# Weight splitting spread over an attention layer's ticks, low parts one block behind, and a differential layer with its memory units first

## The chip, the cores and the metric

The kernel runs on one core of a Trainium2 chip. The metric is the device time of one execution in microseconds. Before the change the median of three runs is 2098.37 us (2098.26 to 2100.83).

## The reference

A transformer of two blocks runs in fp32 on one sequence of 256 rows, width 1024. Cut to what matters here:

```python
def first_block(x, mem, ...):
    mem_n = rmsnorm(mem, mem_norm_g)
    for i in range(2):
        kv = mem_n @ mem_w_kv[i]                                # memory keys and values
        x = x + 0.5 * swiglu(rmsnorm(x, ...), ffn_w_up[i, 0], ffn_w_down[i, 0])
        h = rmsnorm(x, norm_g[i, 1])
        mix = pool_layer(h, ...) if i == 0 else diff_layer(h, ...)
        x = x + mix
        x = x + 0.5 * swiglu(rmsnorm(x, ...), ffn_w_up[i, 1], ffn_w_down[i, 1])
    return rmsnorm(x, final_norm_g)

def diff_layer(h, w_in, lam_p, norm_g, w_out, mem_k, mem_v, slopes, layer_idx):
    proj = h @ w_in                                             # q, k, v, xq
    o = diff_attention(q, k, v, lam, slopes)                    # softmax(c=0) - lam * softmax(c=1), times v
    o = rmsnorm(o, norm_g, eps=SUBLN_EPS) * (1.0 - lam_init)
    xo = memory_attention(xq, mem_k, mem_v)
    return jnp.concatenate([o, xo], axis=-1) @ w_out
...
```

A second block follows: attention with block-sparse heads and heads that keep the top 64 keys by an index score, with a modulation of its norms that comes out of a matrix `w_ada`, and then a layer of product-key experts (the query phase finds the top 16 keys of each half, the expert phase runs over all experts' matrices u and v).

## The kernel before, in words

The program is one straight list of instructions; `manual_schedule` (line 63) keeps the order in which the code emits them on each engine. Nothing is moved by a scheduler, so where a line stands in a generator decides what it waits behind.

**Weights.** Every matrix is stored in blocks of 512 KB (128 x 1024 fp32). `load_to` (L120) issues their loads on SP's queue, five blocks ahead. fp32 products are made of three fp32r matmuls (`mm3`, L184 to L186: high by high, high by low, low by high), so each block is split: `split_one` (L131) lets ACT copy the high part (`whi`, L144) and DVE subtract it from the raw block for the low part (`wlo`, L145). `nextw` (L150) hands out one block and before that splits up to four blocks ahead; `fetch(4)` hands out four, a group's worth, so the four blocks of the next group are split in one burst.

**Order around the change.** In the feed-forward layers a group is `proj_cols` over four blocks: 96 matmuls, with an evacuation by DVE in the middle (`silu`, L520 to L522) and one at the end (`gate`, L532); the next group's `fetch(4)` comes behind that. In the first three feed-forward layers, pieces of `w_ada` stand between the weight blocks in the list `items`; when their turn comes to be split, `ada_piece` (L454) runs two DVE operations instead (`acc`, L463 and L465).

In the pool layer, the differential layer and the second block's attention, `pipeline(units, order)` walks over units (an attention head pair of one row tile each, or a memory head pair) in ticks; a unit is a list of steps s0, s1, ... (scores, softmax, transposes, products), and each tick runs one step of several units in the order given by the second argument. Between ticks a table `counts` says how many yields of the chain `fill` (projections, then the output rows `out_proj_k`) to run. The differential layer fills k0 and q0 first, runs the differential units over k1, q1, v and xq, and ends with the memory units (`mem_units`, L548).

**Names in the rows.** mm and sm are PSUM tiles of matmuls, tr of transposes; hT is the layer's transposed input; mT the transposed memory; cat the concatenated outputs before the output matrix; e a softmax tile; score and m belong to the top-k rounds; sc, v and i to the top-16 jobs of the query phase.

```python
def mm3(out, a, b, start, stop):
    PE.matmul(out, a[0], b[0], start=start, stop=False)
    PE.matmul(out, a[0], b[1], start=False, stop=False)
    PE.matmul(out, a[1], b[0], start=False, stop=stop)
...
drain(qk(k[0]), qk(q[0]))
units = [make(t, h) for g in range(2) for t in range(NT) for h in (4 * g, 4 * g + 2)]
units += mem_units(sp, qx, n4.rstd, KT[1], VV[1], ..., ("k0", "q0", "k1", "q1"))
```

Of the kernel before, what the change touches and what calls it, by code (L numbers as in the profile page):

```python
# [60 lines left out]
def kernel(ctx: ExitStack, tc: tile.TileContext, A, LAY, stop=None):  # L61
# [38 lines left out]


    items = []
    st = {"load": 0, "split": 0, "use": 0, "nsplit": 0, "raw": {}, "s": {}}
    deferred = []
    cfg = {"raw": 5, "ahead": 4}
    CH = 1024
    wpool = ctx.enter_context(pool("wp", side="right"))
    wstack = ctx.enter_context(ExitStack())
# [11 lines left out]
    def load_to(n):  # L120
        while st["load"] < min(n, len(items)):
# [6 lines left out]
            st["raw"][st["load"]] = r  # L128
            st["load"] += 1

    def split_one():  # L131
        j = st["split"]
        load_to(j + cfg["raw"])
        _, nk, w, call = items[j][:4]
        n = nk * w
        r = st["raw"].pop(j)
        if call is not None:
            call(r[:, :n].rearrange("p (k w) -> p k w", w=w))
        else:
            p_ = wpool2 if j < dense and st["nsplit"] % 2 else wpool  # L140
            st["nsplit"] += 1
            hi = p_.tile([P, CH], F32R, name="whi", tag="whi", bufs=4)
            lo = p_.tile([P, CH], F32R, name="wlo", tag="wlo", bufs=4)
            ACT.activation(hi[:, :n], r[:, :n], AF.Copy)  # L144
            V.tensor_tensor(lo[:, :n], r[:, :n], hi[:, :n].bitcast(F32), op=OP.subtract)  # L145
            st["s"][j] = Split(hi[:, :n].rearrange("p (k w) -> p k w", w=w), lo[:, :n].rearrange("p (k w) -> p k w", w=w))
        st["split"] += 1
        load_to(j + 1 + cfg["raw"])

    def nextw():  # L150
        while items[st["use"]][3] is not None:
            st["use"] += 1
        j = st["use"]
        ahead, k = 0, j + 1
        while k < len(items) and ahead < cfg["ahead"]:
            ahead += items[k][3] is None
            k += 1
        while st["split"] < k:
            split_one()
        st["use"] += 1  # L160
        return st["s"].pop(j), items[j][1], items[j][2]

    def split_more(n):
        for _ in range(n):
# [59 lines left out]
    def proj_cols(act, n, n_ct, evac):  # L224
        got = fetch(n)
        for c0 in range(0, n_ct, 2):
            p = pmm()
            m = min(2, n_ct - c0)
            for j in range(m):
                if j:  # L230
                    yield
                proj_col(act, got, c0 + j, p[:, j * S:(j + 1) * S])
            evac(c0, m, p[:, :m * S].rearrange("p (j t) -> p j t", t=S))
            yield
        run_deferred()

# [157 lines left out]
    def out_proj_k(segs, update, nxt, tail=2, ahead=None):  # L394


        p = [[pmm() for _ in range(2)] for _ in range(NT)]
        n = len(segs)

        def mm(t, h, gis, gots):  # L400
            for gi in gis:
                act, k0 = segs[gi]
                for c, k, _ in gots[gi][h]:
                    mm3(p[t][h], act[:, k0 + k, t * P:(t + 1) * P], c[:, k, :], gi == 0 and k == 0, gi == n - 1 and k == 1)

        gots = {}
        for gi in range(n - tail):
            gots[gi] = [fetch(1), fetch(1)]
            for t in range(NT):
                for h in range(2):  # L410
                    mm(t, h, [gi], gots)
                if t:
                    run_deferred()
                yield
        was = dict(cfg)
        cfg.update(ahead=8 - 2 * tail)
        for gi in range(n - tail, n):
            gots[gi] = [fetch(1), fetch(1)]
        cfg.update(was)
        for t in range(NT):  # L420
            for h in range(2):
                cut = n - 1 if nxt.deep and t and h else n
                mm(t, h, range(n - tail, cut), gots)
                if cut < n:
                    was = dict(cfg)
                    cfg.update(ahead=0)
                    ahead.append(fetch(4))
                    nxt.realT(0)
                    mm(t, h, range(cut, n), gots)
                    if tail > 2:  # L430
                        split_more(1)
                update(t, h, p[t][h])
                nxt.pre(t, h)
                if not nxt.deep and (t or h):
                    nxt.T(*((0, 0), (0, 1), (1, 0))[2 * t + h - 1])
                if h:
                    nxt.stats(t)
                if cut < n:
                    ahead.append(fetch(4))
                    cfg.update(was)  # L440
                yield
        if not nxt.deep:
            nxt.late = [lambda: nxt.T(1, 1)]
# [101 lines left out]

    XS = 128 ** -0.5

    def mem_units(sp, qT, rstd, kT, v, dst, tags):  # L548

        turn = itertools.cycle(tags)  # L550

        def make(hp, t):
            e = {}

            def s0():
# [6 lines left out]
                mx, nb, sm, rc = (small([P, 2], x, bufs=6) for x in ("mx", "nb", "sum", "rc"))  # L562
                V.tensor_reduce(mx, pv, axis=AX.X, op=OP.max)
                V.tensor_scalar(nb, mx, rs, -1.0, op0=OP.mult, op1=OP.mult)
                ee = sp.tile([P, 2, S], F32, name="e", tag=next(turn), bufs=1)
                for j in range(2):
                    ACT.activation(ee[:, j], pv[:, j], AF.Exp, bias=nb[:, j:j + 1], scale=rs, accum_out=sm[:, j:j + 1])
                e["e"], e["s"], e["r"] = ee, sm, rc
# [181 lines left out]
        return dump(xt)  # L750

    n2 = Norm(A["norm_g"][0, 2])
    with pool("pl") as sp:
        cat = Split(sp.tile([P, 12, S], F32R, name="cat_hi"), sp.tile([P, 12, S], F32R, name="cat_lo"))
        pb = sp.tile([P, 4, 384], F32, name="poolB")
# [6 lines left out]
        def u_part(h):  # L762
            got = fetch(4)
            for t in range(NT):
                n1.before(t)
                p = pmm()
                rows_mm(p, hT, got[:4], t, 0, 512, 8)
                yield
                rows_mm(p, hT, got[4:], t, 0, 512, 8)
                ACT.activation(u[t][:, h * 512:(h + 1) * 512], p, AF.Copy, scale=n1.rstd[:, t:t + 1])  # L770
                if t:
                    run_deferred()
                yield

        def pooled(c0):
# [8 lines left out]
        def mixed():  # L784
# [4 lines left out]
            for ct in range(8):  # L789
                g, db = ct // 2, ct % 2  # L790
                p = psm()[:, :S]
                for cb in range(2):
                    col = cb * S + db * P
                    mm3(p, wg[g][0][:, g % 2, col:col + P], hT[:, 2 * g + cb, :], cb == 0, cb == 1)
                split_evac(cat[:, ct, :], p, psc[:, ct:ct + 1])
                if ct % 2:
                    yield

        drain(u_part(0), proj_cols(hT, 4, 4, lambda c0, m, p: ACT.activation(qT[:, c0:c0 + m, :], p, AF.Copy)))
# [3 lines left out]
        for n, _ in zip(counts, pipeline(units, [(1, 2), (3, 3), (None, 0), (0, 0), (2, 2)])):  # L803
            for _ in range(n):
                step(fill)
        drain(fill)
    kv0.close()
    if stop == "pool":
        return dump(xt)
# [9 lines left out]


    n5 = Norm(A["norm_g"][1, 2])
    with pool("df") as sp:
        cat = Split(sp.tile([P, 12, S], F32R, name="cat_hi"), sp.tile([P, 12, S], F32R, name="cat_lo"))
        nd = sp.tile([P, S], F32, name="nd")
# [97 lines left out]
        def v_part(h):  # L922

            got = fetch(4)
            for t in range(NT):
                n4.before(t)
                p = pmm()
                rows_mm(p, hT, got[:4], t, 0, 512, 8)
                yield
                rows_mm(p, hT, got[4:], t, 0, 512, 8)  # L930
                ACT.activation(v[:, t, h * 512:(h + 1) * 512], p, AF.Copy, scale=n4.rstd[:, t:t + 1])
                if t:
                    run_deferred()
                yield

        drain(v_part(0))
# [2 lines left out]
        def qk(dst):  # L939
            return proj_cols(hT, 4, 4, lambda c0, m, p: V.tensor_tensor(dst[:, c0:c0 + m, :], p, rbb, op=OP.mult))  # L940

        drain(qk(k[0]), qk(q[0]))
        units = [make(t, h) for g in range(2) for t in range(NT) for h in (4 * g, 4 * g + 2)]
        units += mem_units(sp, qx, n4.rstd, KT[1], VV[1], Split(cat.hi[:, 8:, :], cat.lo[:, 8:, :]), ("k0", "q0", "k1", "q1"))
        o = out_proj_k([(cat, i) for i in range(0, 12, 2)], plain_add, n5)
        fill = itertools.chain(qk(k[1]), qk(q[1]), v_part(1),
                               proj_cols(hT, 4, 4, lambda c0, m, p: ACT.activation(qx[:, c0:c0 + m, :], p, AF.Copy)), o)
        counts = [1] * 9 + [2, 0, 1, 0, 0, 2, 1, 1, 1, 0, 0] + [1, 0] * 2 + [1, 1, 0, 1, 0, 2]
        for i, _ in enumerate(pipeline(units, [(5, 6), (1, 2), (4, 4), (None, 0), (6, 6), (0, 0), (3, 3), (2, 2)])):
            for _ in range(counts[i] if i < len(counts) else 1):  # L950
                step(fill)
        drain(o)
    kv1.close()
    if stop == "diff":
        return dump(xt)
# [45 lines left out]
        return dump(xt)  # L1001


    gotv, got = m1.got
    mvp = [pmm() for _ in range(NT)]
    iqp, ixp = pmm(), psm()
# [93 lines left out]
    def v_part():  # L1100
        got = fetch(4)
        for t in range(NT):
            p = pmm()
            rows_mm(p, hT, got[:4], t, 0, 512, 8)
            yield
            rows_mm(p, hT, got[4:], t, 0, 512, 8)
            ACT.activation(av[:, t, 512:], p, AF.Copy)
            if t:
                run_deferred()
            yield  # L1110

    def make(t, g):
# [88 lines left out]
        return dump(xt)  # L1201


    got = m2.got
    def q_rows(b, t):
        p = pmm()
# [87 lines left out]
    for f in late_scores:  # L1294
        f()
    q1st.close()
    wstack.close()
    pq2 = pqst.enter_context(pool("pq2"))

# [252 lines left out]
def _np_layout(inputs):  # L1552
# [36 lines left out]
    lay["pool_w_group"] = [(0, 2, 512), (P * 1024, 2, 512)]  # L1589
    pack("pool_w_out", g["pool_w_out"][0], None, order=range(6))  # L1590
    w = g["diff_w_in"][0]
    pack("diff_w_in", np.concatenate([w[:, 2048:2560], w[:, 1024:1536], w[:, :512], w[:, 1536:2048], w[:, 512:1024], w[:, 2560:]], 1),
         [512] * 7)
    pack("diff_w_out", g["diff_w_out"][0], None, order=range(6))
    pack("w_ada", g["w_ada_2"][0], [512] * 12)
    w = g["w_in_2"][0]
    w = np.concatenate([w[:, 1024:1536], w[:, 3072:], w[:, :1024], w[:, 1536:3072]], 1)
# [37 lines left out]
```

## Time and profile before

| | us |
|---|---|
| median of three runs | 2098.37 |
| the profiled execution | 2098.71 |
| its span | 2096.9 |
| PE busy | 2033.5 |
| DVE busy | 1458.4 |
| ACT busy | 985.5 |

The span runs from the first to the last instruction; the execution's time is 1.8 us longer. The stages in the trace, by their start: memory keys and values 0, first feed-forward layer 48, pool layer 279, two feed-forward layers 375, differential layer 780, fourth feed-forward layer 875, the second block's norm 1088 and attention 1122, query phase 1260, expert phase 1318. To read such a profile, look first at how busy TensorE is in each stage, then at what it waits for where it isn't, and then, on the engine that releases it, at what stood ahead of the late instruction. The mean granted TensorE clock of the execution is 0.987.

### The profile page before, as it was taken

What the parts mean: (1) busy time and instruction counts of PE and PEld (TensorE: products, weight loads), DVE (VectorE), ACT (ScalarE), POOL (GpSimd) and SP (SyncE); (2) the same over time, 40 slices, a digit from 0 to 9 for tenths busy, and PEclk for the clock granted to TensorE, in tenths of its full rate; (3) what the DMA queues carried; (4) which work ended last, traced back from release to release, by engine and by line L of the source; (5) the groups of instructions that cost most, each with busy time, mean ns of one, the idle gap of its engine ahead of it and who ended that gap; (6) DMA issues with size and microseconds to landing.
All of it is one profiled execution on the core that took longest, in us unless ns stands there. A gap on an engine that the chain in (4) does not pass through costs nothing. (4 is left out here: it accounts for less than half of the span.)

```text
span 2096.9 us, 34488 instructions
## 1 busy us (share of the span) xinstructions
PE 2033.5 (97%) x13678; PEld 1832.0 (87%) x13678; DVE 1458.4 (70%) x2330; ACT 985.5 (47%) x1508; POOL 39.0 (2%) x74
## 2 busy tenths in 40 slices
PE   8999999999999998899989899999999999999998
PEld 7999888998999797799878779999998888888886
DVE  6677566776677568756658688889976666666666
ACT  6444454444444445354444344455554444444444
POOL 2000000000000000000000000000000000000000
PEclk9999999999999999999999899999999999999999
DMA  7667535676576552355545333556676776777764
GB/s 274 217 236 266 188 134 205 227 250 233 185 248 244 187 195 101 120 191 198 206 124 180 104 98 134 175 178 213 245 252 209 226 231 207 225 243 225 225 211 140
DMA packets 142379, 416.93 MB, mean 199 GB/s; under 512 B 12469, under 2 KB 47429, under 8 KB 140041
## 3 DMA queue, kind: packets, MB, share of 16 engines
q1 hardware_dynamic: 102672, 372.04, 52.4%
q10 hardware_dynamic: 37976, 36.91, 5.5%
q0 software_dynamic: 1568, 5.77, 0.9%
q8 instruction: 107, 1.75, 0.3%
q14 instruction: 56, 0.45, 0.1%
HBM read 396.82 MB, written 17.86 MB: 198 GB/s over the span
## 5 line engine op out<-in xcount | busy, mean ns | idle before, releaser
L145 DVE TENSOR_TENSOR wlo<-raw,whi 128x1024 fp32r<-128x1024 f32 (+1 forms) x654 | 780.6, 1222 | 329.8 <-ACT whi L144 329.5
L144 ACT ACTIVATE whi<-raw 128x1024 fp32r<-128x1024 f32 (+1 forms) x654 | 663.0, 1048 | 147.6 <-PE mm L186 85.4
L184 PE MATMUL mm<-hT_hi,whi 128*128 128x256 f32 x1680 | 479.9, 286 | 0.0
L185 PE MATMUL mm<-hT_lo,whi 128*128 128x256 f32 x1680 | 473.1, 282 | 0.0
L186 PE MATMUL mm<-hT_hi,wlo 128*128 128x256 f32 x1680 | 472.9, 281 | 0.0
L184 PEld LDWEIGHTS mm<-hT_hi,whi 128*128 128x128 f32 x1680 | 319.0, 190 | 6.5 <-issue 6.1
L185 PEld LDWEIGHTS mm<-hT_lo,whi 128*128 128x128 f32 x1680 | 318.9, 190 | 2.0 <-issue 1.9
L186 PEld LDWEIGHTS mm<-hT_hi,wlo 128*128 128x128 f32 x1680 | 318.7, 190 | 0.0
L184 PE MATMUL sm<-hT_hi,whi 128*128 128x256 f32 (+1 forms) x1048 | 299.5, 286 | 5.4 <-DVE hT_hi L192 2.2
L186 PE MATMUL sm<-hT_hi,wlo 128*128 128x256 f32 (+1 forms) x1048 | 296.5, 283 | 4.4 <-DVE wlo L145 4.4
L185 PE MATMUL sm<-hT_lo,whi 128*128 128x256 f32 (+1 forms) x1048 | 296.1, 283 | 0.4 <-DVE hT_lo L195 0.4
L184 PEld LDWEIGHTS sm<-hT_hi,whi 128*128 128x128 f32 (+1 forms) x1048 | 199.2, 190 | 8.7 <-DVE hT_hi L192 2.6
L184 PE MATMUL mm<-whi,wh 128*128 128x512 f32 x512 | 204.1, 399 | 2.1 <-ACT wh L194 2.1
L186 PEld LDWEIGHTS sm<-hT_hi,wlo 128*128 128x128 f32 (+1 forms) x1048 | 199.2, 190 | 4.8 <-DVE wlo L145 4.8
L186 PE MATMUL mm<-whi,wl 128*128 128x512 f32 x512 | 202.2, 395 | 0.0
L185 PEld LDWEIGHTS sm<-hT_lo,whi 128*128 128x128 f32 (+1 forms) x1048 | 199.3, 190 | 2.8 <-DVE hT_lo L195 0.6
L185 PE MATMUL mm<-wlo,wh 128*128 128x512 f32 x512 | 201.5, 394 | 0.0
L194 ACT ACTIVATE wh<-wf 128x256 fp32r<-128x256 f32 x128 | 53.5, 418 | 215.6 <-DVE wf L1484 215.6
L184 PE MATMUL mm<-whi,gT_hi 128*128 128x512 f32 x352 | 140.0, 398 | 0.0
L186 PE MATMUL mm<-whi,gT_lo 128*128 128x512 f32 x352 | 139.5, 396 | 0.0
L185 PE MATMUL mm<-wlo,gT_hi 128*128 128x512 f32 x352 | 138.6, 394 | 0.0
L1316 ACT ACTIVATE act<-sm 128x256 f32<-128x256 f32 x128 | 49.1, 384 | 166.3 <-PE sm L186 166.3
(308 smaller groups left out, 2615.9 us busy)
## 6 DMA issues: line engine op xcount, KB each, us to landing
raw<-in_ffn_up_dram SPq DMA_DIRECT2D x176, 512.0 KB, 5.2
raw<-in_peer_u_dram SPq DMA_DIRECT2D x128, 512.0 KB, 3.7
raw<-in_peer_v_dram SPq DMA_DIRECT2D x128, 512.0 KB, 3.8
raw<-in_ffn_dn_dram SPq DMA_DIRECT2D x88, 512.0 KB, 5.2
raw<-in_w_ada_dram SPq DMA_DIRECT2D x48, 512.0 KB, 5.0
gall<-stage ACTq DMA_DIRECT2D x16, 1024.0 KB, 4.6
G<-gall ACTq DMA_DIRECT2D x16, 1024.0 KB, 7.2
raw<-in_diff_w_in_dram SPq DMA_DIRECT2D x28, 512.0 KB, 5.5
```

What stands on the lines that cost most here:

```text
L144: ACT.activation(hi[:, :n], r[:, :n], AF.Copy)
L145: V.tensor_tensor(lo[:, :n], r[:, :n], hi[:, :n].bitcast(F32), op=OP.subtract)
L184: PE.matmul(out, a[0], b[0], start=start, stop=False)
L185: PE.matmul(out, a[0], b[1], start=False, stop=False)
L186: PE.matmul(out, a[1], b[0], start=False, stop=stop)
L194: ACT.activation(hi, src, AF.Copy)
L1316: ACT.activation(act[n], p, AF.Gelu)
```

## The change

Three edits.

1. Everywhere, `split_one` emits only the high part and notes the block in `st["low"]`; the low part of a block is emitted one block later (`low_one`), or at once when the item split is a piece of `w_ada`, or when `nextw` hands out the block. The prefetch runs as many blocks shorter as there are low parts open.
2. In the pool layer, the differential layer and the second block's attention `cfg["spread"]` is set: `nextw` splits nothing ahead, and `ahead_one()` at each yield of the projections and output rows splits one block, at most four ahead.
3. In the differential layer the xq projection and the memory units come first, the differential units after; the columns of `diff_w_in` and rows of `diff_w_out` are packed in the new order, and `counts` is new.

```diff
+    def low_one():
+        j, r, p_ = st["low"].pop(0)
+        c = st["s"][j]
+        nk, w = items[j][1:3]
+        lo = p_.tile([P, CH], F32R, name="wlo", tag="wlo", bufs=4)
+        V.tensor_tensor(lo[:, :nk * w], r[:, :nk * w], c.hi.rearrange("p k w -> p (k w)").bitcast(F32), op=OP.subtract)
+        c.lo = lo[:, :nk * w].rearrange("p (k w) -> p k w", w=w)
...
     def split_one():
         j = st["split"]
-        load_to(j + cfg["raw"])
+        load_to(j + cfg["raw"] - len(st["low"]))
...
             hi = p_.tile([P, CH], F32R, name="whi", tag="whi", bufs=4)
-            lo = p_.tile([P, CH], F32R, name="wlo", tag="wlo", bufs=4)
             ACT.activation(hi[:, :n], r[:, :n], AF.Copy)
-            V.tensor_tensor(lo[:, :n], r[:, :n], hi[:, :n].bitcast(F32), op=OP.subtract)
-            st["s"][j] = Split(hi[:, :n].rearrange("p (k w) -> p k w", w=w), lo[:, :n].rearrange("p (k w) -> p k w", w=w))
+            st["s"][j] = Split(hi[:, :n].rearrange("p (k w) -> p k w", w=w), None)
+            st["low"].append((j, r, p_))
         st["split"] += 1
-        load_to(j + 1 + cfg["raw"])
+        while len(st["low"]) > 1 or st["low"] and call is not None:
+            low_one()
+        load_to(j + 1 + cfg["raw"] - len(st["low"]))
...
-        while k < len(items) and ahead < cfg["ahead"]:
+        while k < len(items) and ahead < cfg["ahead"] and not cfg["spread"]:
...
         while st["split"] < k:
             split_one()
+        while st["s"][j].lo is None:
+            low_one()
...
+    def ahead_one():
+        if cfg["spread"] and st["split"] < min(st["use"] + 4, len(items)):
+            split_one()
...
                 if j:
+                    ahead_one()
                     yield
...
-        drain(qk(k[0]), qk(q[0]))
-        units = [make(t, h) for g in range(2) for t in range(NT) for h in (4 * g, 4 * g + 2)]
-        units += mem_units(sp, qx, n4.rstd, KT[1], VV[1], Split(cat.hi[:, 8:, :], cat.lo[:, 8:, :]), ("k0", "q0", "k1", "q1"))
-        o = out_proj_k([(cat, i) for i in range(0, 12, 2)], plain_add, n5)
-        fill = itertools.chain(qk(k[1]), qk(q[1]), v_part(1),
-                               proj_cols(hT, 4, 4, lambda c0, m, p: ACT.activation(qx[:, c0:c0 + m, :], p, AF.Copy)), o)
-        counts = [1] * 9 + [2, 0, 1, 0, 0, 2, 1, 1, 1, 0, 0] + [1, 0] * 2 + [1, 1, 0, 1, 0, 2]
+        drain(proj_cols(hT, 4, 4, lambda c0, m, p: ACT.activation(qx[:, c0:c0 + m, :], p, AF.Copy)))
+        units = mem_units(sp, qx, n4.rstd, KT[1], VV[1], Split(cat.hi[:, 8:, :], cat.lo[:, 8:, :]), ("e",), 6)
+        units += [make(t, h) for g in range(2) for t in range(NT) for h in (4 * g, 4 * g + 2)]
+        o = out_proj_k([(cat, i) for i in (8, 10, 0, 2, 4, 6)], plain_add, n5)
+        fill = itertools.chain(qk(k[0]), qk(q[0]), qk(k[1]), qk(q[1]), v_part(1), o)
+        counts = [1] * 16 + [1, 1, 1, 0, 1, 1, 1, 1, 0, 1, 1, 0, 1, 1, 0, 1] + [1, 0, 1, 1]
...
+    while st["low"]:
+        low_one()
     wstack.close()
```

The order that comes of it, at three places (the changed kernel's lines are shifted: L145 is now L137, L465 is L488, L532 is L555, L680 and L683 are L703 and L706, L1090 and L1091 are L1122 and L1123).

DVE at the start, while the first memory group waits for its weights; before:

```order
4 L680 TENSOR_TENSOR xg<-tr,cols 128x512 x2
5 L145 TENSOR_TENSOR wlo<-raw,whi 128x1024
6 L683 TENSOR_TENSOR mT_lo<-xg,mT_hi 128x4x128
7 L680 TENSOR_TENSOR xg<-tr,cols 128x512
8 L683 TENSOR_TENSOR mT_lo<-xg,mT_hi 128x4x128
9 L680 TENSOR_TENSOR xg<-tr,cols 128x512
10 L683 TENSOR_TENSOR mT_lo<-xg,mT_hi 128x4x128 x2
11 L145 TENSOR_TENSOR wlo<-raw,whi 128x1024 x3
```

and now:

```order
4 L703 TENSOR_TENSOR xg<-tr,cols 128x512 x2
5 L706 TENSOR_TENSOR mT_lo<-xg,mT_hi 128x4x128
6 L703 TENSOR_TENSOR xg<-tr,cols 128x512
7 L706 TENSOR_TENSOR mT_lo<-xg,mT_hi 128x4x128
8 L703 TENSOR_TENSOR xg<-tr,cols 128x512
9 L706 TENSOR_TENSOR mT_lo<-xg,mT_hi 128x4x128 x2
10 L137 TENSOR_TENSOR wlo<-raw,whi 128x1024 x4
```

The first low part has moved from ahead of the four mT_lo to behind them.

DVE at a group's end in the first feed-forward layer, where a piece of `w_ada` is next; before:

```order
L507 TENSOR_TENSOR gT_lo_698<-gate_921,gT_hi_697 128x512
L532 TENSOR_TENSOR gate_1056<-mm_1007,silu_924 128x512
L465 SCALAR_TENSOR_TENSOR acc_797<-raw_929,cols_79,acc_797 128x512 x2
L145 TENSOR_TENSOR wlo_1065<-raw_933,whi_1064 128x1024
L145 TENSOR_TENSOR wlo_1071<-raw_939,whi_1070 128x1024
L145 TENSOR_TENSOR wlo_1077<-raw_945,whi_1076 128x1024
```

and now:

```order
L530 TENSOR_TENSOR gT_lo_694<-gate_917,gT_hi_693 128x512
L555 TENSOR_TENSOR gate_1052<-mm_1003,silu_920 128x512
L488 SCALAR_TENSOR_TENSOR acc_793<-raw_931,cols_79,acc_793 128x512 x2
L137 TENSOR_TENSOR wlo_1058<-raw_925,whi_943 128x1024
L137 TENSOR_TENSOR wlo_1068<-raw_933,whi_1064 128x1024
L137 TENSOR_TENSOR wlo_1074<-raw_941,whi_1066 128x1024
```

Behind the piece now stands the low part of a block whose high part (`whi_943`) was made in the burst before. PE takes that block as the last of the four of the group it has just begun:

```order
564 L203 MATMUL mm_1088<-hT_lo_68,whi_937 128x256
565 L204 MATMUL mm_1088<-hT_hi_67,wlo_945 128x256
566 L202 MATMUL mm_1088<-hT_hi_67,whi_943 128x256 [waits Activation_49]
567 L203 MATMUL mm_1088<-hT_lo_68,whi_943 128x256
568 L204 MATMUL mm_1088<-hT_hi_67,wlo_1058 128x256 [waits DVE_49]
569 L202 MATMUL mm_1088<-hT_hi_67,whi_943 128x256
```

DVE in the second block's attention, between the top-k rounds (four MAX and four MATCH_REPLACE each) that follow the index score; before, the second round and what follows it:

```order
690 L1090 MAX m_11303<-score 128x8
691 L1091 MATCH_REPLACE score<-m_11303,score 128x128
692 L1090 MAX m_11306<-score 128x8
693 L1091 MATCH_REPLACE score<-m_11306,score 128x128
694 L1090 MAX m_11309<-score 128x8
695 L1091 MATCH_REPLACE score<-m_11309,score 128x256
696 L1090 MAX m_11312<-score 128x8
697 L1091 MATCH_REPLACE score<-m_11312,score 128x256
698 L145 TENSOR_TENSOR wlo<-raw,whi 128x1024 x4
```

and now:

```order
704 L1118 TENSOR_TENSOR score<-score,fut 128x256
705 L137 TENSOR_TENSOR wlo<-raw,whi 128x1024
706 L1122 MAX m_11256<-score 128x8
707 L1123 MATCH_REPLACE score<-m_11256,score 128x128
708 L1122 MAX m_11259<-score 128x8
709 L1123 MATCH_REPLACE score<-m_11259,score 128x128
710 L1122 MAX m_11262<-score 128x8
711 L1123 MATCH_REPLACE score<-m_11262,score 128x256
712 L1122 MAX m_11265<-score 128x8
713 L1123 MATCH_REPLACE score<-m_11265,score 128x256
714 L137 TENSOR_TENSOR wlo<-raw,whi 128x1024
```

Four low parts in a row have become one between each two rounds.

## Rows read from the trace of the kernel before

**Rows 1.** The page, part 1: busy us (share of the span) of each engine, instructions.
```profile
PE 2033.5 (97%) x13678; PEld 1832.0 (87%) x13678; DVE 1458.4 (70%) x2330; ACT 985.5 (47%) x1508; POOL 39.0 (2%) x74
```

**Rows 2.** Windows: stretch and its length, busy us (instructions) by engine, PEclk, DMA share, GB/s.
```profile
50.00:279.00 229.00, 229.00 (x1578) 211.63 (x1577) 152.02 (x182) 101.58 (x125) 2.17 (x4) 1.00 0.64 222
...
279.00:375.00 96.00, 93.62 (x548) 81.33 (x548) 65.20 (x100) 49.46 (x77) 2.65 (x3) 1.00 0.47 161
...
780.00:875.00 95.00, 81.04 (x502) 69.98 (x501) 73.53 (x179) 45.96 (x128) 4.07 (x4) 0.95 0.29 100
...
1122.00:1260.00 138.00, 125.25 (x784) 104.84 (x782) 109.90 (x255) 60.14 (x131) 2.60 (x3) 0.93 0.37 122
...
1260.00:1318.00 58.00, 52.85 (x390) 50.25 (x391) 50.61 (x252) 24.66 (x34) 0.43 (x1) 0.97 0.36 126
```

**Rows 3.** Waits of PE, whole span: engine line waited for, total us, times, longest.
```profile
PE tr L243 <- DVE cat_lo L201: 5.1, 2, 4.3
...
PE sm L186 <- DVE wlo L145: 4.4, 2, 3.9
...
PE tr L243 <- DVE e L1152: 3.8, 1, 3.8
...
PE tr L243 <- DVE qr L1256: 1.5, 1, 1.5
```

**Rows 4.** Windows again: two stretches right behind long waits.
```profile
1173.90:1180.70 6.80, 6.80 (x28) 5.96 (x29) 5.16 (x15) 2.08 (x8) 0.00 (x0) 0.50 0.41 145
...
1314.00:1317.30 3.30, 3.09 (x14) 3.09 (x15) 3.30 (x9) 0.00 (x0) 0.00 (x0) 0.50 0.68 191
```

**Rows 5.** Timeline of DVE at the start: start us, us, operation, count, [idle <-releaser].
```profile
8.88 1.23 DVE L145 TENSOR_TENSOR wlo<-raw,whi 128x1024 fp32r<-128x1024 f32 x1 [1.64 <-ACT whi L144]
...
12.42 1.47 DVE L683 TENSOR_TENSOR mT_lo<-xg,mT_hi 128x512 fp32r<-128x512 f32 x2
```

**Rows 6.** Timeline of PE at the start.
```profile
11.53 0.63 PE L185 MATMUL mm<-wlo,mT_hi 128*128 128x512 f32 x1
```

**Rows 7.** Timeline of PE: matmul 21 of the first kT group.
```profile
26.25 0.28 PE L186 MATMUL mm<-mT_hi,wlo 128*128 128x256 f32 x1
```

**Rows 8.** Timeline of DVE around the same group.
```profile
27.96 0.15 DVE L249 TENSOR_SCALAR ms<-ss 128x1 f32<-128x1 f32 x1
```

**Rows 9.** Timeline of DVE at a group end in the first feed-forward layer.
```profile
95.14 0.68 DVE L532 TENSOR_TENSOR gate<-mm,silu 128x512 f32<-128x512 f32 x1
...
95.74 1.53 DVE L465 SCALAR_TENSOR_TENSOR acc<-raw,cols,acc 128x512 f32<-128x512 f32 x2
```

**Rows 10.** Timeline of PE there: first matmul of the next group, and its matmul 21.
```profile
94.96 0.28 PE L184 MATMUL mm<-hT_hi,whi 128*128 128x256 f32 x1
...
97.31 0.28 PE L186 MATMUL mm<-hT_hi,wlo 128*128 128x256 f32 x1
```

**Rows 11.** The page, part 5 (mean ns of one) and part 6 (us to landing).
```profile
L145 DVE TENSOR_TENSOR wlo<-raw,whi 128x1024 fp32r<-128x1024 f32 (+1 forms) x654 | 780.6, 1222 | 329.8 <-ACT whi L144 329.5
...
raw<-in_ffn_up_dram SPq DMA_DIRECT2D x176, 512.0 KB, 5.2
```

**Rows 12.** Timeline of DVE in the differential layer.
```profile
816.47 4.63 DVE L145 TENSOR_TENSOR wlo<-raw,whi 128x1024 fp32r<-128x1024 f32 x4 [0.78 <-ACT whi L144]
```

**Rows 13.** Timeline of PE right behind it.
```profile
822.69 0.66 PE L243 MATMUL tr<-ident,e 128*128 128x128 f32 x2 [4.26 <-DVE cat_lo L201]
```

**Rows 14.** Timeline of DVE in the second block's attention: two successive top-k rounds.
```profile
1130.23 0.29 DVE L1090 MAX8 m<-score 128x8 f32<-128x128 f32 x1
...
1133.38 0.28 DVE L1090 MAX8 m<-score 128x8 f32<-128x128 f32 x1
```

**Rows 15.** Timeline of PE in the same microseconds.
```profile
1134.90 0.28 PE L186 MATMUL mm<-hT_hi,wlo 128*128 128x256 f32 x1
```

**Rows 16.** Timeline of DVE in the query phase: first index searches of two successive jobs.
```profile
1283.46 0.29 DVE L1230 FIND_INDEX8 i<-v,sc 128x8 uint32<-128x128 f32 x1
...
1288.13 0.29 DVE L1230 FIND_INDEX8 i<-v,sc 128x8 uint32<-128x128 f32 x1
```

More of the change, by code (lines that the diff above doesn't have):

```diff
@@ L102 @@
     items = []
-    st = {"load": 0, "split": 0, "use": 0, "nsplit": 0, "raw": {}, "s": {}}
+    st = {"load": 0, "split": 0, "use": 0, "nsplit": 0, "raw": {}, "s": {}, "low": []}
     deferred = []
-    cfg = {"raw": 5, "ahead": 4}
+    cfg = {"raw": 5, "ahead": 4, "spread": False}
     CH = 1024
@@ L233, in proj_cols @@
             evac(c0, m, p[:, :m * S].rearrange("p (j t) -> p j t", t=S))
+            ahead_one()
             yield
@@ L413, in out_proj_k @@
                     run_deferred()
+                ahead_one()
                 yield
@@ L440, in out_proj_k @@
                     cfg.update(was)
+                if not nxt.deep:
+                    ahead_one()
                 yield
@@ L546, with mem_units @@
     XS = 128 ** -0.5
-    def mem_units(sp, qT, rstd, kT, v, dst, tags):
+    def mem_units(sp, qT, rstd, kT, v, dst, tags, bufs=1):
         turn = itertools.cycle(tags)
@@ L564, in s0 @@
                 V.tensor_scalar(nb, mx, rs, -1.0, op0=OP.mult, op1=OP.mult)
-                ee = sp.tile([P, 2, S], F32, name="e", tag=next(turn), bufs=1)
+                ee = sp.tile([P, 2, S], F32, name="e", tag=next(turn), bufs=bufs)
                 for j in range(2):
@@ L752 @@
     n2 = Norm(A["norm_g"][0, 2])
+    cfg["spread"] = True
     with pool("pl") as sp:
@@ L767, in u_part @@
                 rows_mm(p, hT, got[:4], t, 0, 512, 8)
+                ahead_one()
                 yield
@@ L772, in u_part @@
                     run_deferred()
+                ahead_one()
                 yield
@@ L796, in mixed @@
                 if ct % 2:
+                    ahead_one()
                     yield
@@ L806 @@
         drain(fill)
+    cfg["spread"] = False
     kv0.close()
@@ L821 @@
     n5 = Norm(A["norm_g"][1, 2])
+    cfg["spread"] = True
     with pool("df") as sp:
@@ L928, in v_part @@
                 rows_mm(p, hT, got[:4], t, 0, 512, 8)
+                ahead_one()
                 yield
@@ L933, in v_part @@
                     run_deferred()
+                ahead_one()
                 yield
@@ L952 @@
         drain(o)
+    cfg["spread"] = False
     kv1.close()
@@ L1001 @@
         return dump(xt)
+    cfg["spread"] = True
     gotv, got = m1.got
@@ L1104, in v_part @@
             rows_mm(p, hT, got[:4], t, 0, 512, 8)
+            ahead_one()
             yield
@@ L1109, in v_part @@
                 run_deferred()
+            ahead_one()
             yield
@@ L1201 @@
         return dump(xt)
+    cfg["spread"] = False
     got = m2.got
@@ L1591, in _np_layout @@
     w = g["diff_w_in"][0]
-    pack("diff_w_in", np.concatenate([w[:, 2048:2560], w[:, 1024:1536], w[:, :512], w[:, 1536:2048], w[:, 512:1024], w[:, 2560:]], 1),
+    pack("diff_w_in", np.concatenate([w[:, 2048:2560], w[:, 3072:], w[:, 1024:1536], w[:, :512], w[:, 1536:2048], w[:, 512:1024], w[:, 2560:3072]], 1),
          [512] * 7)
-    pack("diff_w_out", g["diff_w_out"][0], None, order=range(6))
+    pack("diff_w_out", g["diff_w_out"][0], None, order=(4, 5, 0, 1, 2, 3))
     pack("w_ada", g["w_ada_2"][0], [512] * 12)
```

## Prediction

> **What bounds the kernel now.** I read the page first. TensorE is busy for 97% of the span [rows 1], so a stretch can gain only where TensorE waits or is clocked down. The view of windows shows where that is [rows 2]. In the feed-forward stretch from 50 to 279 us PE is busy 229.00 of 229.00 us: no gain is to be had there, and anything new that PE waits for costs its full length. The pool layer has 96.00 - 93.62 = 2.4 us of idle PE, the differential layer 95.00 - 81.04 = 14.0, the second block's attention 138.00 - 125.25 = 12.8, the query phase 58.00 - 52.85 = 5.2. The same rows show PEclk 0.95, 0.93 and 0.97 in the last three. One minus the mean clock, times the length, is the time lost to the lower clock: 0.05 x 95 = 4.8, 0.07 x 138 = 9.7, 0.03 x 58 = 1.7 us. So everything in reach is 2.4 + 18.8 + 22.5 + 6.9, some 50 us or 2.4%.
>
> The view of PE's waits says who is late [rows 3]: in the differential layer cat_lo (one wait of 4.3 us), in the second block e of L1152 (3.8), in the query phase a low part itself (3.9 of 4.4). The timeline shows why: cat_hi and cat_lo stand on VectorE (DVE) behind a burst of four low parts, 4.63 us long [rows 12], and PE idles 4.26 us right behind it [rows 13]. Behind such a wait the granted clock is 0.50, the 1.2 GHz level, for some microseconds [rows 4]. The wait of 1.5 us for qr [rows 3] has no such price: the 1.7 us lost in the query phase [rows 2] is half of the single 3.3 us at 0.50 that follows the 3.9 us wait [rows 4].
>
> **The change, part by part.** PE, DVE and ScalarE (ACT) execute the same instructions as before; only places move. The sum is made against the profiled execution, 2098.71 us (span 2096.9 and 1.8 around it), 0.3 us above the median of the runs, 2098.37.
>
> *Low parts one block behind, start.* Before, the first wlo runs at 8.88 us, ahead of the last two mT_lo, which end at 12.42 + 1.47 = 13.9 [rows 5]; PE first uses it at 11.53 [rows 6]. Now it stands behind them: 13.9 + 1.2 = 15.0, so PE waits 15.0 - 11.5 = **+3.4**. In the first kT group the last block's low part moves behind the statistics, which end at 28.1 [rows 8], so it ends at 29.3; matmul 21 wants it at 26.25 [rows 7]: **+3.1**. These statistics follow PE's earlier work through ACT, so they move along with the first delay; if they didn't, this one would be hidden. Bounds 3.4 to 8 (more, if PE restarts at the lower clock).
>
> *Low parts one block behind, feed-forward layers.* Each group takes four blocks, and the last block's low part now stays back until the next fetch, whose code comes behind the gate operation. In the rows, gate starts 0.18 us after the group's first matmul, at 94.96, and matmul 21, the first to use that part, starts at 97.31, 2.35 later [rows 9, 10]. Where the low part follows gate directly it runs from 95.74 and is done near 96.9: 0.4 us to spare, nothing lost. But at nine boundaries (three in each of the first three feed-forward layers) the next item is a piece of w_ada: two acc operations, to 95.74 + 1.53 = 97.27 [rows 9], come first, and the low part is done at 97.27 + 1.2 = 98.5. PE waits 1.2 each, 9 x 1.2 = **+10.8**. PE has no idle time here to hide it [rows 2]. The clock I leave alone, since 1.5 us did not lower it. Bounds: 9.9 without the semaphore's time, 17 if the two dozen other boundaries lose their margin.
>
> *Loads.* Each prefetch goes out one low part (1.22 us) later on SP's queue. It lands 5.2 us after issue [rows 11], and a group of 96 matmuls at 0.117 us (2.35 over 20 steps [rows 10]) lasts 11.3 us: nothing. Without that cover, at most 1.2 a group. The memory units' larger e pool and the reordered columns and rows of the weights cost nothing at run time; POOL's and ACT's queues gain no work.
>
> *Pool layer.* The bursts go; the first group boundary pays for a high part that now comes after an evacuation. **-1**, between -2.4 and +1.
>
> *Differential layer.* All 14.0 us of waits and 4.8 of clock were tied to bursts or to the chains of its units; I let all go, -18.8. In their place: with one split per yield, the last two blocks of a group are split only around the group's end. ACT's high part, then DVE's evacuation (0.68, as gate), the low part of the block before (1.2), the unit's own step and the last low part (1.2) must fit in the 2.35 us to matmul 21. A short unit step of some 0.8 us overruns by 0.8 to 1.8, a differential unit's step of 2 us by 2.5: five boundaries, 7.5 together. In the middle ticks DVE is the full engine (73.5 of 95 us in the whole stretch [rows 2], the first part of it light), and three of them cost 3.8. At the end the output rows now wait for the last differential unit, whose cat parts stand behind an add, an xg, an hT_lo, statistics and a low part: 4.3, and 1.0 more at the next layer's first rows. Sum 16.6, and two drops of the clock, 4: **+1.8**. Bounds: -18.8 if all is covered; +12 if every place drops the clock.
>
> *Second block's attention.* Four bursts of four or two go, with 12 of the 12.8 us and the 9.7 of clock: -21.7. New: at the border of the aq and ak columns two low parts stand each behind a top-k round of 1133.38 - 1130.23 = 3.15 us [rows 14]. The score is done at 1130.3; low part, round, low part, round, low part end at 1130.3 + 3 x 1.2 + 2 x 3.15 = 1140.1, where PE wants the last at 1134.90 [rows 15]: +5.2, and the clock drops once, 1.7. Three more boundaries by the same reckoning as above 4.1, ikT and remnants 2.4, one more drop 1.3: +14.7. Net **-7**, between -21.7 and +5. The rows show that a burst costs PE what stands behind it [rows 12, 13]. The Trainium skill (Perfetto Trace Analysis, Optimizing Scalar/DVE Operations) goes further: where such an engine is not saturated but makes others idle, breaking its work up may let it finish sooner. By that rule alone both layers would keep their full gain, -18.8 and -21.7, and the sum would be some 35 us lower. The trace agrees on DVE's share, 70% over the span.
>
> *Query phase.* One last low part waits behind a top-16 job, 1288.13 - 1283.46 = 4.67 us [rows 16], overrunning by 2.2; another behind three jobs, overrunning by 4. The old 3.9 us wait, caused by the same full DVE, goes: **+2.3**, between -4 and +7.
>
> Sum: 3.4 + 3.1 + 10.8 - 1 + 1.8 - 7 + 2.3 = +13.4, so 2098.7 + 13.4 = **2112**.
>
> **Rivals.** *A, the bursts were the whole loss.* PE has other ready work at the new boundaries, so the 16.6 + 4 and the 14.7 don't arise: 13.4 - 20.6 - 14.7 = -21.9, **2077**. It decides at the boundary: if DVE reaches the last low part within 2.35 us of a group's first matmul. For it: of PE's listed waits only 4.4 us are for a low part itself [rows 3]. Against: PE's order is fixed, so the group's next matmul is all it may run. Half of A gives 2094. *B, exchange:* the losses are just balanced by the two layers, which give 13 us more than I think: **2098**. For it, the range of the two layers, 31 and 27 us wide. *C, the clock:* each 1.2 us wait in the feed-forward layers also drops the clock, 1.7 each, 9 x 1.7 = 15: **2128**. Against it stands the 1.5 us wait without a drop. That bursts remain despite the edit isn't one: the new order has the low parts singly between the units' steps.
>
> **How the numbers follow.** Forecast 0.6, A in full or in part 0.2, B 0.12, C or other extra losses 0.08. The range takes in B, the better half of A, and the forecast with its upper bounds short of C: 2091 to 2127, which leaves out about half of A and half of C. A measurement can tell 0.2%, about 4.2 us, from no change: faster 0.20, same 0.13, slower 0.67 (the forecast's own low tail adds a little to same).
>
> **What would show it.** Right: a PE wait of about 3 us for wlo near 11.5 us, nine PE waits of about 1.2 us for wlo in the first three feed-forward layers, and one of 5 us between aq and ak; no burst of four low parts between 780 and 1260 us. Wrong: PE still fully busy from 50 to 279 us (my 10.8 falls), or under 8 us idle in the differential layer and 6 in the second block's (A).

## The result, and the profile after

The changed kernel takes 2125.99 us (median of four runs, 2122.28 to 2128.36); the kernel before, run beside it, 2098.32. The ratio is 1.0129, with an interval of 1.0108 to 1.0149: 27.7 us slower. The forecast was 2112, slower; the measured time lies inside the range, 1 us below its upper end of 2127, at twice the forecast loss; two of the four single runs (2128.36 and 2128.33) lie above that end. The profiled execution took 2128.36 us, 29.65 more than the profiled one of before.

The page of the changed kernel, part 1, answers to [rows 1]:

```profile
PE 2040.6 (96%) x13678; PEld 1834.9 (86%) x13678; DVE 1442.7 (68%) x2330; ACT 982.5 (46%) x1508; POOL 43.7 (2%) x74
```

The counts are the same. PE is busy 7 us longer and the span is 29.6 us longer, so most of the loss is new waiting. The waits of PE over the whole span, answering to [rows 3]:

```profile
PE mm L204 <- DVE wlo L137: 27.6, 23, 3.4
PE mm L202 <- DVE hT_hi L210: 10.8, 2, 7.1
...
PE mm L203 <- DVE wlo L137: 7.0, 4, 3.2
PE sm L204 <- DVE wlo L137: 4.8, 5, 1.8
PE mm L202 <- DVE cat_hi L216: 4.0, 1, 4.0
...
PE sm L202 <- ACT act L1353: 2.5, 1, 2.5
PE tr L263 <- DVE cat_lo L219: 2.3, 1, 2.3
```

A low part is now what PE waits for most: 27.6 + 7.0 + 4.8 = 39.4 us in 32 waits, where before it was 4.4. The waits of 4.3 and 4.6 us for cat_lo and rc (the reciprocals of the softmax sums) in the differential layer are down to 2.3 or gone; one of 7.1 us for hT_hi is new.

**Where the time went.** PE runs 13,678 matmuls in both kernels, so both can be cut at the same matmul number, here a little behind each layer's first rows. (The stage starts listed ahead of the prediction are rough, and some lie well inside a layer: by the tiles that PE reads, the pool layer lies between the last rows on gT at 251 us and the last on cat at 343, the differential layer between 730 and 891. The windows of the prediction hold most of these layers' waits, not their whole length.) Differences to the profiled execution of before, in us, for the change and for five runs of the next section:

| stage (number of the matmul it is cut at) | before | change | 1 alone | 2 alone | 3 alone | 2 and 3 | 1 in three layers |
|---|---|---|---|---|---|---|---|
| start (0) | 71.49 | +9.13 | +8.98 | +0.26 | +0.12 | +0.13 | +0.08 |
| three feed-forward layers (372, 2194, 3508) | 578.24 | +11.45 | +11.36 | +0.23 | 0.00 | +1.02 | -0.16 |
| pool layer (1696) | 92.41 | +3.70 | -0.91 | +6.69 | +0.01 | +6.69 | +0.35 |
| differential layer (4822) | 161.19 | +2.85 | -1.73 | +11.49 | +3.69 | +13.41 | -1.67 |
| fourth feed-forward layer (5776) | 180.32 | +1.28 | 0.00 | +1.28 | 0.00 | +1.28 | 0.00 |
| second block's norm (7014) | 43.17 | -2.07 | -0.66 | +0.26 | +0.13 | -1.29 | -0.14 |
| its attention (7224) | 134.19 | -2.99 | -8.45 | +6.27 | -2.52 | +7.88 | -10.87 |
| query phase (7976) | 57.04 | +3.02 | +3.02 | -0.25 | +0.63 | -0.56 | +0.19 |
| expert phase, first part (8366) | 97.65 | +4.85 | +3.83 | -0.67 | +1.43 | -0.38 | 0.00 |
| the rest, to the last matmul (9190) | 671.90 | -1.62 | -0.67 | +2.53 | -0.51 | +2.25 | +1.72 |

"1" is the low parts one block behind, "2" the spread splitting, "3" the new order; "2 and 3" is low_now, "1 in three layers" late_in_layers_alone. "3 alone" also shows how far a stage moves that isn't touched at all: 2.5 us in the second block's attention, 1.4 in the expert phase. Other untouched stages move by up to 1.0 (the three feed-forward layers in "2 and 3") and 2.5 us (the rest in "2 alone"). Single differences of that size are not to be read.

### The profile page after: what moved, and what is told of

Its sections match the earlier page's. It is cut to its first block, busy times and chain, and to the rows that moved or that the text cites. A ratio compares the mean times of both kernels' runs of the same rounds, so it can differ in the third digit from the quotient of the medians.

```text
span 2126.5 us, 34242 instructions
## 1 busy us (share of the span) xinstructions
PE 2040.6 (96%) x13678; PEld 1834.9 (86%) x13678; DVE 1442.7 (68%) x2330; ACT 982.5 (46%) x1508; POOL 43.7 (2%) x74
## 4 chain that ended last, share of the span: by engine, by line
PE 86%; DVE 10%; ACT 2%; issue 1%; DMA 1%; ACTq 0%; POOL 0%; POOLq 0%; DVEq 0%; SPq 0%
PE mm L204 21%; PE mm L202 21%; PE mm L203 21%; PE sm L204 5%; PE sm L202 5%; PE sm L203 5%; DVE wlo L137 4%; PE mm L1471 2%; PE tr L263 1%; ACT junk L273 1%; ACT whi L153 1%; DVE i L1265 1%; DVE v L1263 0%; PE sm L1158 0%; PE tr L611 0%
## 5 line engine op out<-in xcount | busy, mean ns | idle before, releaser
L137 DVE TENSOR_TENSOR wlo<-raw,whi 128x1024 fp32r<-128x1024 f32 (+1 forms) x654 | 779.1, 1219 | 134.6 <-ACT whi L153 134.0
L213 DVE TENSOR_TENSOR wl<-wf,wh 128x256 fp32r<-128x256 f32 x128 | 54.5, 425 | 198.5 <-ACT wh L212 198.5
```

Source lines behind the costliest of these rows:

```text
L137: V.tensor_tensor(lo[:, :nk * w], r[:, :nk * w], c.hi.rearrange("p k w -> p (k w)").bitcast(F32), op=OP.subtract)
L213: V.tensor_tensor(lo, src, hi.bitcast(F32), op=OP.subtract)
```

## The experiments

My theory T after reading the result: the late low parts are the whole loss, since the stages outside the three spread layers account for 9.1 + 11.5 + 3.0 + 4.9 = 28.5 us. The rival S: the spread splitting and the order lose the time. Each edit was tried alone, and the first was taken away from the change.

**Without the first edit (low_now).**

```diff
-        while len(st["low"]) > 1 or st["low"] and call is not None:
+        while st["low"]:
             low_one()
```

> The change without its first edit: every low part is subtracted right behind its high part again; the spread splitting and the new order of the differential layer stay. Theory T (the late low parts are the loss: start 9 us, three feed-forward layers 11.5, query phase 3, expert phase 5, in sum 28): 2126 - 28 = 2098 us or a little less, 2086 to 2100, and no PE wait for wlo in the feed-forward layers. Rival S (the spread splitting and the new order are the loss, and the late low parts only show where it is felt): 2112 to 2126.

Measured: 2127.31 us, ratio to before 1.0126 [1.0102, 1.0149]. T falls. Start, feed-forward layers, query and expert phase do go back to before, to within some 1 us, as T said of them; but pool, differential and second block's attention lose 6.7 + 13.4 + 7.9 = 28.0 us, which the late low parts had kept down to 3.6.

**The first edit alone (late_low_alone)**: `cfg["spread"]` stays False, and the old order is kept.

> The kernel before with the first edit alone: low parts one block behind, bursts and the old order kept. T: 2098 + 28 = 2126, 2120 to 2132, with nine PE waits of about 1.0 us in the first three feed-forward layers and the start 9 us longer. S: 2098 to 2108.

Measured: 2110.77 us, 1.0052 [1.0032, 1.0072]. Neither theory's figure. The losses outside the three layers come as T says, 27.2 us by the table (9.0 + 11.4 + 3.0 + 3.8); within the three layers the edit *gains* 11.1, 8.5 of it in the second block's attention.

**The second edit alone (spread_alone)**: low parts at once, the old order.

> The kernel before with the second edit alone: one split per yield in the pool layer, the differential layer and the second block's attention, low parts at once, the old order of units. T: the bursts' waits go, the group boundaries and one burst of four at the end of the second block's output rows come: 2088 to 2102. S: 2105 to 2120.

Measured: 2125.32 us, 1.0121 [1.0097, 1.0145]: slower than S expected. The waits of DVE for ACT's high part in the differential layer (total us, times, longest) are, first in the kernel before, then in this one, then in old_order (further down), which is this one with the late low parts:

```profile
DVE wlo L145 <- ACT whi L144: 11.2, 5, 5.9
```

```profile
DVE wlo L137 <- ACT whi L153: 26.4, 17, 4.0
```

```profile
DVE wlo L137 <- ACT whi L153: 5.5, 2, 2.9
```

With the new order of units, the same waits are in low_now, and with the late low parts, in the changed kernel:

```profile
DVE wlo L137 <- ACT whi L153: 31.9, 14, 4.8
```

```profile
DVE wlo L137 <- ACT whi L153: 11.6, 5, 4.0
```

The timeline of DVE in spread_alone shows two of the 17 waits, and that of PE what stands behind them:

```profile
805.28 1.23 DVE L137 TENSOR_TENSOR wlo<-raw,whi 128x1024 fp32r<-128x1024 f32 x1 [1.71 <-ACT whi L153]
...
815.97 2.36 DVE L137 TENSOR_TENSOR wlo<-raw,whi 128x1024 fp32r<-128x1024 f32 x2 [4.04 <-ACT whi L153]
```

```profile
808.10 0.74 PE L263 MATMUL tr<-ident,e 128*128 128x128 f32 x4 [2.17 <-DVE e L901]
...
819.92 1.09 PE L263 MATMUL tr<-ident,e 128*128 128x128 f32 x4 [2.19 <-DVE e L901]
```

ACT reaches the high part only after the unit's exponentials and what stands behind them (804.20 and 814.89 in its timeline); DVE, whose next instruction is that block's low part, stands until it is there; the unit's softmax comes behind, and PE's transposes wait for it five times, 8.1 us in all:

```profile
PE tr L263 <- DVE e L901: 8.1, 5, 2.2
```

A burst pays such a wait once for several blocks (5 waits), the spread splitting 17 times. With the low part one block behind, DVE works on a block whose high part is long there: 26.4 us of waiting become 5.5 with the old order, 31.9 become 11.6 with the new one. So the first two edits belong together in these layers, where edit 1 is worth some 24 us on top of 2 and 3 (28.0 to 3.6), and even that only makes good the damage of 2.

**The third edit alone (order_alone)**: bursts, low parts at once, memory units first.

> The kernel before with the third edit alone: memory units first in the differential layer, output rows reordered, bursts kept, low parts at once. T: nothing outside the differential layer moves; within it the end waits about 4 us for the last unit's cat parts and the bursts stay: 2095 to 2104. S (the order is the loss): 2105 or more.

Measured: 2101.94 us, 1.0014 [1.0003, 1.0024]. The differential layer takes 3.7 us more.

From here the theory was U: the late low part gains where ACT is late, and costs where DVE's own queue ahead of the delayed part is long. It asks for the first edit in the three layers alone.

**The first edit in the three layers, without spread and new order (late_in_layers_alone)**: `cfg["late"]` is 1 in those layers and 0 elsewhere.

```diff
-        while len(st["low"]) > 1 or st["low"] and call is not None:
+        while len(st["low"]) > cfg["late"] or st["low"] and call is not None:
             low_one()
```

> The kernel before with low parts one block behind in the pool layer, the differential layer and the second block's attention alone; bursts, old order, and everywhere else low parts at once. Theory U (the first edit pays where ACT's high part is late and DVE would stand waiting for it, and costs where DVE's queue ahead of the delayed part is long): the three layers keep what the first edit alone showed in them, -0.9, -1.7 and -8.5, and the costs elsewhere go: 2098.5 - 11 = 2087, 2083 to 2092. Rival V (stage lengths shift with the phase of the clock, the gains are luck): 2095 to 2101.

Measured: 2088.86 us, 0.9948 [0.993, 0.9967], 10 us faster than before and 37 faster than the change. V falls as an account of the whole: the slowest of the four runs, 2090.40, is 7 us under the fastest of the fourteen of before, 2097.61. The gain is in the second block's attention; the windows of that stage, first of before, then of this kernel:

```profile
1126.80:1261.00 134.20, 121.37 (x753) 101.72 (x753) 106.27 (x250) 57.23 (x124) 2.60 (x3) 0.92 0.35 117
```

```profile
1125.30:1248.60 123.30, 113.11 (x754) 94.33 (x753) 106.92 (x251) 57.20 (x124) 2.60 (x3) 1.00 0.38 127
```

PE's idle time falls only from 12.8 to 10.2 us, but its busy time from 121.4 to 113.1 for the same matmuls: the mean granted clock is 1.00, not 0.92. DVE's waits for ACT's high part in that stage fall from 5.1 to 1.9 us. Behind this burst of before PE had waited 3.8 us [rows 3] and then run 6.8 us at 1.2 GHz [rows 4]:

```profile
1167.88 4.63 DVE L145 TENSOR_TENSOR wlo<-raw,whi 128x1024 fp32r<-128x1024 f32 x4 [2.30 <-ACT whi L144]
```

Now DVE first takes the part held back from the burst before, while ACT makes the high parts, and three in a row follow (first fence, DVE); PE waits twice, briefly (second fence):

```profile
1162.22 1.22 DVE L137 TENSOR_TENSOR wlo<-raw,whi 128x1024 fp32r<-128x1024 f32 x1
1164.61 3.50 DVE L137 TENSOR_TENSOR wlo<-raw,whi 128x1024 fp32r<-128x1024 f32 x3 [1.17 <-ACT whi L153]
```

```profile
1163.49 0.38 PE L204 MATMUL mm<-hT_hi,wlo 128*128 128x256 f32 x1 [1.51 <-DVE wlo L137]
...
1168.56 0.92 PE L263 MATMUL tr<-ident,e 128*128 128x128 f32 x4 [0.92 <-DVE e L1187]
```

**The same with the second block's attention spread (second_block_spread)**, and its last fetch split ahead as before.

> As late_in_layers_alone, but the second block's attention is spread too, and the last fetch of its output rows splits the query weights ahead again, so that no burst of four stands before the transposed rows. U: that stage gives what the changed kernel's gave, -3.0, and the 7.1 us wait and its clock drop besides, -13 in all, so 2083, 2079 to 2088. V: 2095 or more.

Measured: 2090.09 us, 0.9954 [0.994, 0.9968]. A miss, 2 us above the range: that stage gives 7.8, not 13, and no more than without the spread. Two waits between the aq and ak columns, of 0.85 and 3.31 us, stay.

**The change with low parts at once outside the three layers (late_low_in_layers).**

```diff
-        while len(st["low"]) > 1 or st["low"] and call is not None:
+        while len(st["low"]) > 1 or st["low"] and (call is not None or not cfg["spread"]):
             low_one()
```

> The changed kernel with low parts at once wherever the splitting isn't spread. U: start, feed-forward layers, query and expert phase return to before, 9.1 + 11.4 + 3.0 + 4.8 = 28 us less than 2126: 2098, 2093 to 2102. V: 2105 or more.

Measured: 2104.13 us, 1.0021 [1.0012, 1.0031]. Between U's range and V's, 2 us above the one and under 1 below the other; by stages start, feed-forward layers, query and expert phase are each within 0.6 us of before. What is left is the price of edits 2 and 3 with the late low parts: 3.8 in the pool layer, 3.3 in the differential layer, 1.3 behind it, against 3.1 gained in the second block.

**Query weights split ahead again (tail_ahead).**

```diff
-        cfg.update(ahead=8 - 2 * tail)
+        cfg.update(ahead=8 - 2 * tail, spread=cfg["spread"] and not nxt.deep)
```

> The changed kernel in which the last fetch of the second block's output rows splits the query weights ahead as before the change, in place of four in a row right before the transposed rows. U: the PE wait of 7.1 us for hT_hi goes, and half-clock time behind it, 1.7 to 3.4: 2126 - 9 = 2117, 2114 to 2120. If something else set that wait (the row's statistics, a load): 2122 to 2128.

Measured: 2116.81 us, 1.0078 [1.0059, 1.0096], by the median as U said. The wait doesn't go altogether: it falls from 7.12 to 1.91 us. The profiled execution is the slowest of the four, 2123.00 us, 5.4 under the profiled one of the change, 3.4 of it in this stage; where the other 4 us of the medians lie isn't shown. In the changed kernel this is the burst (DVE, then PE):

```profile
1263.01 4.63 DVE L137 TENSOR_TENSOR wlo<-raw,whi 128x1024 fp32r<-128x1024 f32 x4 [1.80 <-ACT whi L153]
1267.56 0.16 DVE L363 SCALAR_TENSOR_TENSOR ma<-mod,cols 128x8 f32<-128x8 f32 x1
1267.82 1.36 DVE L375 TENSOR_SCALAR xg<-tr,ma,mod 128x128 f32<-128x128 f32 x4
1269.22 0.43 DVE L210 CAST hT_hi<-xg 128x512 fp32r<-128x512 f32 x1
```

```profile
1269.79 0.77 PE L202 MATMUL mm<-whi,hT_hi 128*128 128x512 f32 x1 [7.12 <-DVE hT_hi L210]
```

The spread never splits more than is asked for by a yield, and the last part of the output rows has none; so the query phase's four blocks, split ahead in the kernel before, are split when they are fetched, right ahead of the rows that PE needs next.

**An open low part before a piece of w_ada, not behind it (low_before_piece).**

```diff
         if call is not None:
+            while st["low"]:
+                low_one()
             call(r[:, :n].rearrange("p (k w) -> p k w", w=w))
```

> The changed kernel in which an open low part goes out before a piece of w_ada instead of behind it. If the nine PE waits of 1.0 us in the first three feed-forward layers come from the 1.53 us of the piece's two operations ahead of the part, all nine go and these layers return to within 1 us of before each: 2126 - 9 to 11 = 2116, 2113 to 2120. If it is the fetch itself or the shorter prefetch that makes the part late: 2123 to 2128.

Measured: 2113.87 us, 1.0062 [1.0045, 1.0079]. All nine waits are gone, and the three layers stand at -0.02, -0.23 and +0.07 us to before. The piece's two operations ahead of the part are the cause.

**The change with the old order (old_order).**

> The changed kernel with the old order of the differential layer (the first two edits alone). U: without the memory units first, the 4.0 us wait for cat_hi at the end and the 1.2 us of the next layer's first rows go, other waits in that layer stay: 2126 - 5 = 2121, 2117 to 2124. If the new order serves the spread splitting, as its moved fill suggests, taking it away costs: 2127 to 2132.

Measured: 2124.96 us, 1.0114 [1.0097, 1.0131], 1 us under the change by the medians, too little to tell. The wait for cat_hi goes, but one of 3.9 us for a low part comes in its place, and the layer takes 165.2 us (164.0 with the new order). By the profiled executions the new order costs the layer 3.7 us by itself, 1.9 with the spread and low parts at once (13.41 against 11.49), and nothing with both other edits.

## Why the prediction was right, and where it was not

The direction and the range held, the range by 1 us only; the size was off by a factor of two. The mechanism of the two largest losses is shown; the whole goes term by term. The profiled execution loses 29.65 us, 16.2 more than forecast: 4.9 in the expert phase and 1.3 behind the differential layer, where nothing was forecast, 4.7 in the pool layer, 4.0 in the second block's attention, 2.6 at the start. The other stages are off by up to 2.1 us either way.

*Start, +6.5 forecast:* +9.1. The timeline of PE has the first wait as predicted, 3.22 where 3.4 was forecast; the second, in the kT group at 33.3 us, is 2.86 (3.1 forecast), so the two do add up. (From [rows 5, 6] and 1.22 us for a low part, the first comes to 3.6, not 3.4.)

```profile
14.78 0.80 PE L203 MATMUL mm<-wlo,mT_hi 128*128 128x512 f32 x1 [3.22 <-DVE wlo L137]
```

The other 3 us are the clock. The window of the changed kernel behind the second wait reads 0.81, where before it was 1.00 from 13 us on:

```profile
33.00:50.00 17.00, 16.66 (x106) 16.07 (x107) 9.37 (x12) 7.18 (x10) 6.92 (x27) 0.81 0.46 155
```

0.19 x 17 = 3.2 us. That was named as a bound beyond the term, and left out of the term. It doesn't come in every execution: old_order has the same instructions up to there and the same two waits (3.23 and 2.89), its start takes 6.4 us more than before, and its window reads 1.00:

```profile
33.00:50.00 17.00, 16.62 (x118) 15.49 (x119) 12.14 (x14) 8.74 (x12) 6.95 (x27) 1.00 0.59 191
```

So the two waits are the price of the edit, and what the clock adds differs between executions.

*Feed-forward layers, +10.8:* +11.45, nine waits of 0.99 to 1.03 us. Timeline of DVE, then of PE, at the boundary of [rows 9, 10]:

```profile
103.93 0.69 DVE L555 TENSOR_TENSOR gate<-mm,silu 128x512 f32<-128x512 f32 x1 [1.33 <-PE mm L204]
104.54 1.53 DVE L488 SCALAR_TENSOR_TENSOR acc<-raw,cols,acc 128x512 f32<-128x512 f32 x2
105.99 3.49 DVE L137 TENSOR_TENSOR wlo<-raw,whi 128x1024 fp32r<-128x1024 f32 x3
```

```profile
105.96 0.28 PE L203 MATMUL mm<-hT_lo,whi 128*128 128x256 f32 x1
107.26 0.39 PE L204 MATMUL mm<-hT_hi,wlo 128*128 128x256 f32 x1 [1.02 <-DVE wlo L137]
```

The idle time counts from the end of the matmul before, 0.28 us after its start, while matmuls here start 0.12 us apart. From start to start the wait costs 107.26 - 105.96 - 0.12 = 1.2 us, as forecast, and the next start comes 0.1 late; nine such delays make 11.4. The two dozen other boundaries kept their margin, and the clock in this stretch stays at 1.00, as left alone in the sum.

*Second block's attention, -7:* -3.0. The two low parts between top-k rounds come as forecast: DVE takes a low part, 3.1 us of top-k, a low part, in turn, and PE waits 0.85 and 3.31 us (5.2 forecast):

```profile
1165.91 0.58 PE L204 MATMUL mm<-hT_hi,wlo 128*128 128x256 f32 x1 [3.31 <-DVE wlo L137]
```

The step that failed is a dismissal: "That bursts remain despite the edit isn't one". One did, in the fetch of the query weights, and it cost a wait of 7.1 us: 9.2 us by the medians of the change and tail_ahead, 5.4 by their profiled executions. In the two traces without it this stage reads -6.4 (tail_ahead) and -7.8 (second_block_spread), near the forecast. Two more bursts stay at the ends of the pool layer and the differential layer, where the spread ends and the next layer's blocks are fetched; so the sign "no burst of four low parts between 780 and 1260 us" failed too:

```profile
361.20 5.76 DVE L137 TENSOR_TENSOR wlo<-raw,whi 128x1024 fp32r<-128x1024 f32 x5
```

```profile
920.34 5.75 DVE L137 TENSOR_TENSOR wlo<-raw,whi 128x1024 fp32r<-128x1024 f32 x5
```

PE waits 2.0 and 1.2 us for the first part of each (at 362.47 and 921.61).

*Query phase, +2.3:* +3.0. Two waits for a low part behind top-16 jobs came, 1.67 and 3.38 us (2.2 and 4 forecast), and the old one of 3.9 went; the mean clock is 0.94, where it was 0.97 [rows 2].

*Pool layer, -1:* +3.7. I let a burst's wait go and priced one boundary; that wait of 2.0 us for a low part at the next layer's first rows (the kind that I had counted for the differential layer, with 1.0) and the clock behind it were not in the sum. The window there reads 0.84, 0.16 x 11 = 1.8 us:

```profile
362.00:373.00 11.00, 10.53 (x42) 8.48 (x43) 6.13 (x7) 5.51 (x7) 1.36 (x2) 0.84 0.77 285
```

*Differential layer, +1.8:* +2.85. (Another 1.28 us are spread thinly over the groups of the layer behind it in every kernel whose differential layer is spread; their cause was not looked for.) The 4.0 us for cat_hi at the end was forecast as 4.3. But the balance was right for a reason only half seen: I let the bursts' waits vanish because splits came singly, while the runs show that single splits alone add 11.5 us there, and that it is the late low part which takes most of that back.

*Expert phase, nothing forecast:* +4.85. The first u blocks wait 4.4 us in four waits for a low part behind DVE's softmax and gather operations, 2.8 of it in this part of the phase; the clock behind them reads 0.94 from 1440 to 1470 us. The first edit alone shows it too (+3.8), and it goes with the edit. That the look-ahead of only two blocks there makes one block later too late is my reading; a longer one was not tried. I had taken the phase to be covered throughout.

Rival A (the bursts were the whole loss) is refuted: PE is idle for 15.1 us in the differential layer and 15.1 in the second block's attention, where A wanted under 8 and 6. The Trainium skill (Perfetto Trace Analysis, Optimizing Scalar/DVE Operations) says of engines that aren't saturated but hold up others that "breaking up instructions may allow work to be completed sooner". No run here breaks an instruction up; spreading a burst of whole ones, as the prediction read it, makes spread_alone 26.6 us slower. Rival C, a drop of the clock at each 1.2 us wait, did not come: the windows over those layers read 1.00.

## What to carry to other kernels

When one engine's instruction needs another's output, don't put it next in the queue: one block of distance takes away most of the wait for the other engine (26.4 to 5.5 us here), but it pays only where the delayed work isn't then stuck behind longer work of its own engine; ask at each place which of the two is longer. Spreading a burst over ticks turns one wait for the other engine into many (5 into 17 here), so spread only with that distance in place; even then no run here gained over bursts with the same distance (late_in_layers_alone 2088.86, second_block_spread 2090.09). And when a look-ahead is replaced by a rule at yields, search for the fetches that no yield precedes.

## What had not been expected of the hardware

That the clock carries most of a gain: in late_in_layers_alone the second block's attention lost 8.3 us of PE's busy time and only 2.6 of its idle time, when its longest wait fell from 3.8 to 2.2 us. The mean clock of the execution was 0.990 to 0.992 in all four runs, and 0.985 to 0.990 in the fourteen of before.

And that nearly the same waits don't always bring the same clock. In that stage late_low_alone has the same instructions in the same order; its waits over 0.9 us are 2.25, 1.51, 0.93 and 1.91 us, in late_in_layers_alone 2.15, 1.51, 0.92 and 1.91. Yet there the clock reads 0.96, and PE is busy 4.0 us longer than at 1.00:

```profile
1143.90:1269.60 125.70, 117.13 (x753) 98.14 (x753) 107.15 (x251) 57.32 (x124) 2.60 (x3) 0.96 0.38 126
```

Before, with waits of 3.8, 2.4, 2.0 and 1.8, it was 0.92. What decides between them was not tried; so of the 8.3 us some 4 need not come in every execution.
